# Memory keys of a cross-attention kept in DRAM between their making and their use

## Chip, core and metric

One Trainium2 chip, one core. The metric is the device time of one execution in microseconds (us), of which the median of several runs is taken. A profiled execution has a trace of every instruction beside it. Engines are named PE (TensorE), DVE (VectorE), ACT (ScalarE), POOL (GpSimd) and SP (SyncE, which here only issues transfers).

## What is computed

One decoder layer over 512 tokens of width 1024, in float32: a SwiGLU feed-forward block, a mixer (an SSD head group and a differential-attention head group that share one input and one output projection), a cross-attention into a memory of 256 rows, a second feed-forward block, a final norm. The part that the change touches is the cross-attention:

```python
def memory_cross_attention(h, mem_n, w_cq, w_ck, w_cv, w_co):
    bsz, seqlen, _ = h.shape
    mlen = mem_n.shape[1]
    q = (h @ w_cq).reshape(bsz, seqlen, CROSS_HEADS, CROSS_HEAD_DIM)
    k = (mem_n @ w_ck).reshape(bsz, mlen, CROSS_HEADS, CROSS_HEAD_DIM)
    v = (mem_n @ w_cv).reshape(bsz, mlen, CROSS_HEADS, CROSS_HEAD_DIM)
    logits = jnp.einsum('bqhd,bkhd->bhqk', q, k,
                        preferred_element_type=jnp.float32) * (CROSS_HEAD_DIM ** -0.5)
    p = jax.nn.softmax(logits, axis=-1)
    o = jnp.einsum('bhqk,bkhd->bqhd', p.astype(v.dtype), v).reshape(bsz, seqlen, D_MODEL)
    return o @ w_co
```

The keys `k` depend on the memory alone, so they can be made long before the queries.

## The kernel before

**Number format.** PE multiplies in a format (float32r) that keeps fewer bits. So nearly every operand is split into a high and a low part: ACT copies the value into the format (`hi`, line 155 or 159), DVE subtracts that from the value (`lo`, line 156 or 160). A product is three matmuls, hi x hi, hi x lo and lo x hi (`mm3`, which calls `mm`, line 146). Every weight tile is treated so as well: SP loads it raw (`wr`, six buffers, line 174), ACT and DVE split it (`wh`, `wl`, three buffers each).

**Tiles and pools.** Activations lie as tiles of 128 partitions by 512 float32 values (2 KB per partition). They come from one pool, `sp`, with 55 slots of that size (`NSLOT`); tiles of at most 1 KB have 16 slots of their own (`NHALF`). `s2(name)` asks for a tile. A new tile that finds no free slot waits until the last reader of an old one is done. PSUM has eight banks, four under the name `acc` and four under `aux`.

**Stages around the change**, with the times at which the trace shows them:

- 349 to 373 us: `memory_keys` multiplies the memory by `w_ck` into four PSUM banks, two key tiles of 256 columns in each (`pck`).
- 371 to 387 us: `keys_apart` (line 1080) scales each bank by the norm row of the memory into `ckf` (line 1083, DVE) and splits that into two tiles `ck`, a high and a low one. Four banks make eight tiles of 2 KB.
- 373 to 765 us: the mixer. Eight attention heads (`queries_keys`, `head`, `values`, `out_attn`) and four SSD groups (`group_dense`, `group`). The normed input, `hnh` and `hnl`, 16 tiles, is kept until the last gate projection `pz`. A step of its own, `steps` (line 656), turns the time-step projection `pdt` into decays: POOL loads two small constants, `ii` (line 660) and `hb` (line 662), PE turns the projection with `ii` (`pdk`), DVE adds a part of `hb` (line 668), POOL raises e to the other part (`ea`, line 684), DVE uses `ea` at line 685.
- 764 to 814 us: the last output tiles of the attention group and `memory_values`, which makes the values `cv` of the cross-attention (`pcv`).
- 805 to 850 us: `out_proj` multiplies the eight SSD outputs `ys` by the output weights, one output tile of 24 matmuls after the other. `upd_c` (line 1128) adds each to `x`, splits the result for the cross-attention (`h_c`) and sums its squares.
- 850 us on: `cross_dense` makes the queries of a head, `cross` reads `ck` (first at 867 us), and the head's softmax and value product follow.

Beside all this runs `block_sums_in_dram` (line 1243): SP copies weight blocks of the second feed-forward block inside DRAM and POOL adds others onto them (line 1260).

**What sets the order.** `Order` (line 57) runs generators. The dense ones (projections) follow one another; every matmul moves a planner's clock on by its columns plus 8 over 2400, for a tile of 512 columns 0.217 units. The others (`spawn`) are side chains: after each `yield n` a chain becomes due `n` units later and is run between two steps of a dense one. So the code comes out in one long list. SP and POOL execute their part of it exactly in that order:

```python
ctx.enter_context(tc.manual_schedule(engines={mybir.EngineType.SP, mybir.EngineType.Pool}))
```

PE, DVE and ACT get their order from the framework when the program is built: it runs the list through a simulated machine, takes what is ready there, earlier lines first, and hands out the slots of the pools on the way. On the chip every engine then keeps the order it was given.

`keys_apart` starts 1.0 unit after the last key matmul and yields 2.5 after each bank. `steps` starts when `steps_dense` is through, which follows the queries and keys of head 0.

Of the kernel before, what the change touches and what calls it, by code (L numbers as in the profile page):

```python
# [11 lines left out]
F32 = mybir.dt.float32  # L12
# [5 lines left out]
P = 128  # L18
T = 512
D = 1024  # L20
KT = D // P
NF = 22
MEM = 256
# [77 lines left out]
def body(tc, a, dbg=None):  # L101
    nc = tc.nc
# [8 lines left out]
    dram = ctx.enter_context(tc.tile_pool(name="dram", bufs=1, space=bass.MemoryType.DRAM))  # L111
# [3 lines left out]
    def nm(s):  # L115
        uid[0] += 1
        return f"{s}_{uid[0]}"

    def s2(s, dt=F32, shape=(P, T)):
        if math.prod(shape[1:]) <= T // 2:  # L120
            return sp.tile(list(shape), dt, tag="s1", name=nm(s), bufs=NHALF)
        return sp.tile(list(shape), dt, tag="s2", name=nm(s))
# [4 lines left out]
    def small(s, n, bufs=None):  # L127
        return tiny.tile([P, n], F32, tag=s, name=nm(s), bufs=bufs)
# [4 lines left out]
    def aux(s, shape=(P, T)):  # L133
        return aux_p.tile(list(shape), F32, tag="aux", name=nm(s))

    def dump(name, t):
        if dbg and name in dbg:
            nc.sync.dma_start(dbg[name], t.bitcast(F32) if t.dtype == R32 else t)
# [3 lines left out]
    od = Order()  # L142
# [5 lines left out]
    def transpose(out, x):  # L148
        od.t += 2 * (P + 8) / 2400
        nc.tensor.transpose(out, x, ident)  # L150

    def split_into(hi, lo, src, scale=None):
        if scale is None:
            return (
                S.activation(hi, src, AF.Copy),  # L155
                V.tensor_tensor(lo, src, hi.bitcast(F32), ALU.subtract),  # L156
            )
        return (
            S.activation(hi, src, AF.Copy, scale=scale),
            V.scalar_tensor_tensor(lo, src, scale, hi.bitcast(F32), ALU.mult, ALU.subtract),  # L160
        )

    def split(s, src, scale=None, half=False, n=T):
        if half:
            both = s2(s, R32, (P, 2, T // 2))
            hi, lo = both[:, 0], both[:, 1]
        else:
            hi, lo = s2(s + "h", R32, (P, n)), s2(s + "l", R32, (P, n))
        last[:] = [i.ins for i in split_into(hi, lo, src, scale)]
        return hi, lo  # L170
# [145 lines left out]
    def mm3(ps, w, x, first, last, wc=slice(None), xc=slice(None)):  # L316
        (wh, wl), (xh, xl) = w, x
        mm(ps, wh[:, wc], xh[:, xc], first, False)
        mm(ps, wh[:, wc], xl[:, xc], False, False)
        mm(ps, wl[:, wc], xh[:, xc], False, last)  # L320
# [92 lines left out]
    def make_h(k, c, x):  # L413
        return split("hm", x[k], par[:, c + k : c + k + 1])
# [601 lines left out]
    ck, cv = [], []  # L1016
# [52 lines left out]
    def memory_keys():  # L1069
        pairs = []  # L1070
        for n in range(0, KT, 2):
            ps = (aux, acc)[n // 4]("pck", (P, 2, MEM))
            for j in range(2):
                yield from proj(ps[:, j], load_w(a["wck"][n + j]), hm)
            pairs.append(ps)
        hm.clear()
        od.spawn(keys_apart(pairs), 1.0)
        yield lambda: len(h) == KT

    def keys_apart(pairs):  # L1080
        for ps in pairs:
            kf = s2("ckf", shape=(P, 2, MEM))
            V.tensor_tensor(kf, ps, st_mem.row[:, None, :].to_broadcast([P, 2, MEM]), ALU.mult)
            hi, lo = (s2("ck", R32, (P, 2, MEM)) for _ in range(2))
            split_into(hi, lo, kf)
            ck.extend((hi[:, j], lo[:, j]) for j in range(2))
            yield 2.5

    def memory_values():
        pv = [[acc("pcv") for _ in range(2)] for _ in range(2)]  # L1090
# [37 lines left out]
    def upd_c(o, po):  # L1128
        V.tensor_tensor(x[o], x[o], po, ALU.add)
        h_c.append(make_h(o, C_CROSS, x))  # L1130
        st_c.add(x[o])
        dump(f"x2_{o}", x[o])
        if o == KT - 1:
            h.clear()
            od.spawn(islice(st_c.finish(), 1), 3.0)
# [17 lines left out]
    od.add(out_attn(1, SPLIT, 8, True))  # L1153
    od.add(memory_values())
    od.add(out_proj(ys, a["wos"], lambda: all(y is not None for y in ys), upd_c))


    oc = [None] * 8

    def cross_dense(hd):  # L1160
        ps = [acc("pcq") for _ in range(2)]
        for j in range(2):
            yield from proj(ps[j], load_w(a["wcq"][2 * hd + j]), h_c)
        q = [split("cq", ps[j], 0.0625) for j in range(2)]
        od.spawn(cross(hd, q), W["c0"])

    def cross(hd, q):
        pth = [None, None]
        es = [None, None]
        for s in range(3):  # L1170
            if s < 2:
                ps = aux("pcs", (P, 2, MEM))
                for i in range(2):
                    for j in range(2):
                        qs = slice((2 * s + i) * P, (2 * s + i + 1) * P)
                        mm3(ps[:, i], q[j], ck[2 * hd + j], j == 0, j == 1, wc=qs)
                mx = small("cmx", 2)
                V.tensor_reduce(mx, ps, axis=AX.X, op=ALU.max, negate=True)
                col = st_c.col[:, 2 * s : 2 * s + 2]
                V.tensor_tensor(mx, mx, col, ALU.mult)  # L1180
                sm = small("csm", 2)
                e = es[s] = s2("ce", shape=(P, 2, MEM))
                for i in range(2):
                    S.activation(e[:, i], ps[:, i], AF.Exp, bias=mx[:, i : i + 1], scale=col[:, i : i + 1], accum_out=sm[:, i : i + 1])
                rc = small("crc", 2)
                V.reciprocal(rc, sm)
                for i in range(2):
                    V.tensor_scalar(e[:, i], e[:, i], rc[:, i : i + 1], None, ALU.mult)
                yield W["cs"]
            if s > 0:  # L1190
                e = es[s - 1]
                pt = aux("cpt", (P, 2, 2 * P))
                for kb in range(2):
                    for i in range(2):
                        transpose(pt[:, kb, i * P : (i + 1) * P], e[:, i, kb * P : (kb + 1) * P])
                pth[s - 1] = split("pth", pt.rearrange("p a b -> p (a b)"))
                yield W["ct"]
        for j in range(2):
            po = aux("pco")
            f = 2 * hd + j  # L1200
            for i2 in range(2):
                for kb in range(2):
                    mm3(po[:, i2 * 256 : i2 * 256 + 256], cv[kb][f // 4], pth[i2], kb == 0, kb == 1, wc=slice((f % 4) * P, (f % 4 + 1) * P), xc=slice(kb * 256, kb * 256 + 256))
            oc[f] = split("oc", po)
# [366 lines left out]
```

## Time and profile before

| | |
|---|---|
| median of three runs | 1307.42 us (1307.05 to 1309.1) |
| profiled execution | 1307.78 us, of which the span from first to last instruction is 1306.0 us |
| mean granted clock of PE | 0.997 |
| ACT busy | 706.9 us, 54% |
| POOL busy | 120.1 us, 9% |
| bytes moved by transfers | 234.75 MB, mean 180 GB/s |

In the lines of the profile a row such as `L156 DVE TENSOR_TENSOR ck<-ckf,ck x4` names the line of the code, the engine, the operation, the tile written, the tiles read and the count. `[3.96 <-PE pf L146]` behind a row says that the engine had been idle for 3.96 us before it and which event ended that. In the views of waits a row has the waiting instruction, what it waited for, and then the sum in us, the number of times and the longest. A matmul's end is modelled, since matmuls overlap; that PE is busy does not mean that it runs at its peak. Rows of a transfer give the time of its issue; its landing is listed apart.

### The profile page before, as it was taken

What the parts mean: (1) busy time and instruction counts of PE and PEld (TensorE: products, weight loads), DVE (VectorE), ACT (ScalarE), POOL (GpSimd) and SP (SyncE); (2) the same over time, 40 slices, a digit from 0 to 9 for tenths busy, and PEclk for the clock granted to TensorE, in tenths of its full rate; (3) what the DMA queues carried; (4) which work ended last, traced back from release to release, by engine and by line L of the source; (5) the groups of instructions that cost most, each with busy time, mean ns of one, the idle gap of its engine ahead of it and who ended that gap; (6) DMA issues with size and microseconds to landing.
All of it is one profiled execution on the core that took longest, in us unless ns stands there. A gap on an engine that the chain in (4) does not pass through costs nothing.

```text
span 1306.0 us, 20077 instructions
## 1 busy us (share of the span) xinstructions
PE 1288.3 (99%) x7709; PEld 1125.4 (86%) x7709; DVE 972.6 (74%) x1542; ACT 706.9 (54%) x1208; POOL 120.1 (9%) x149
## 2 busy tenths in 40 slices
PE   9999999999999999999999999999999999999997
PEld 7889998997887778777788878888889999989995
DVE  6987898798776676567867687645677878877886
ACT  7554564565754564346645465434365646555564
POOL 0001010001100011101012021020001000000000
PEclk9999999999999999999999999999999999999999
DMA  9367677877974525653475648684248876666653
GB/s 340 87 185 193 185 193 197 229 196 212 284 235 146 138 65 151 226 164 105 91 202 160 193 122 241 189 223 128 65 131 247 208 233 177 189 195 181 186 189 107
DMA packets 69263, 234.75 MB, mean 180 GB/s; under 512 B 8160, under 2 KB 9664, under 8 KB 68816
## 3 DMA queue, kind: packets, MB, share of 16 engines
q1 hardware_dynamic: 53200, 180.91, 41.8%
q0 software_dynamic: 13168, 45.67, 19.4%
q10 hardware_dynamic: 2800, 6.91, 1.6%
q8 instruction: 60, 0.98, 0.3%
q14 instruction: 35, 0.29, 0.1%
HBM read 231.30 MB, written 48.29 MB: 214 GB/s over the span
## 4 chain that ended last, share of the span: by engine, by line
PE 79%; issue 13%; DVE 3%; ACT 2%; POOL 1%; DMA 1%; ACTq 0%; POOLq 0%; DVEq 0%
PE qb L243 12%; PE pm L146 10%; PE qa L243 8%; PE qe L243 8%; PE ob L1294 5%; PE pxbc L146 4%; PE oa L1294 4%; PE oe L1294 3%; PE pcq L146 3%; PE pz L146 3%; PE pa L146 2%; PE pcv L146 2%; PE pg L146 2%; PE pu L146 2%; PE pq L146 2%
## 5 line engine op out<-in xcount | busy, mean ns | idle before, releaser
L155 ACT ACTIVATE wh<-wr 128x1024 fp32r<-128x1024 f32 (+1 forms) x323 | 328.2, 1018 | 331.9 <-issue 63.7
L156 DVE TENSOR_TENSOR wl<-wr,wh 128x1024 fp32r<-128x1024 f32 (+1 forms) x323 | 377.7, 1174 | 133.6 <-ACT wh L155 130.4
L771 ACT ACTIVATE ec<-ec,mn 128x512 f32<-128x512 f32 (+3 forms) x64 | 35.3, 554 | 33.7 <-DVE mn L770 33.7
L146 PE MATMUL pxbc<-hnh,wh 128*128 128x512 f32 x128 | 52.6, 411 | 0.0
L146 PE MATMUL pxbc<-hnh,wl 128*128 128x512 f32 x128 | 50.2, 392 | 0.0
L146 PE MATMUL pxbc<-hnl,wh 128*128 128x512 f32 x128 | 50.2, 392 | 0.0
L243 PE MATMUL qa<-hmh,wl 128*128 128x256 f32 x152 | 43.1, 284 | 0.1
L243 PE MATMUL qe<-s24h,wl 128*128 128x256 f32 x152 | 43.1, 284 | 0.0
L243 PE MATMUL qa<-h11h,wh 128*128 128x256 f32 x152 | 43.1, 283 | 0.0
L243 PE MATMUL qb<-s24h,wl 128*128 128x256 f32 x152 | 43.1, 283 | 0.0
L243 PE MATMUL qb<-s31h,wh 128*128 128x256 f32 x152 | 43.0, 283 | 0.0
L243 PE MATMUL qb<-s31l,wh 128*128 128x256 f32 x152 | 43.0, 283 | 0.0
L243 PE MATMUL qb<-s31h,wl 128*128 128x256 f32 x152 | 43.0, 283 | 0.0
L243 PE MATMUL qa<-h11h,wl 128*128 128x256 f32 x152 | 43.0, 283 | 0.0
L243 PE MATMUL qa<-hmh,wh 128*128 128x256 f32 x152 | 43.0, 283 | 0.0
L243 PE MATMUL qa<-h11l,wh 128*128 128x256 f32 x152 | 43.0, 283 | 0.0
L243 PE MATMUL qa<-hml,wh 128*128 128x256 f32 x152 | 43.0, 283 | 0.0
L243 PE MATMUL qb<-s24l,wh 128*128 128x256 f32 x152 | 43.0, 283 | 0.0
L243 PE MATMUL qe<-s24h,wh 128*128 128x256 f32 x152 | 43.0, 283 | 0.0
L243 PE MATMUL qe<-s24l,wh 128*128 128x256 f32 x152 | 43.0, 283 | 0.0
L243 PE MATMUL qb<-s24h,wh 128*128 128x256 f32 x152 | 43.0, 283 | 0.0
L243 PE MATMUL qb<-hml,wh 128*128 128x256 f32 x152 | 43.0, 283 | 0.0
(457 smaller groups left out, 4170.9 us busy)
## 6 DMA issues: line engine op xcount, KB each, us to landing
wr<-in_f2q SPq DMA_DIRECT2D x44, 512.0 KB, 4.5
wr<-in_f1q SPq DMA_DIRECT2D x40, 512.0 KB, 4.5
wr<-in_f1b SPq DMA_DIRECT2D x25, 512.0 KB, 6.3
isum<-in_f2q SPq DMA_DIRECT2D x22, 512.0 KB, 5.3
wr<-isum SPq DMA_DIRECT2D x22, 512.0 KB, 4.3
wsum<-in_f2b SPq DMA_DIRECT2D x20, 512.0 KB, 6.3
wr<-wsum SPq DMA_DIRECT2D x20, 512.0 KB, 4.9
wr<-in_f1q POOLq DMA_DIRECT2D x16, 512.0 KB, 6.9
```

The lines of the kernel that those rows point to most:

```text
L146: newest_mm[:] = [nc.tensor.matmul(out, w, x, start=start, stop=stop).ins]
L155: S.activation(hi, src, AF.Copy),
L156: V.tensor_tensor(lo, src, hi.bitcast(F32), ALU.subtract),
L243: newest_mm[:] = [nc.tensor.matmul(out, a_[:, wc], b_, start=first and f == 0 and kp == 0 and j == 0, stop=kp == n - 1 and j == 2, skip_gr ...
L771: S.activation(ec[:, :n], ec[:, :n], AF.Exp, bias=mn, scale=-1.0, accum_out=sm[c][:, i : i + 1])
L1294: newest_mm[:] = [nc.tensor.matmul(ps, a_[:, ts], b_[:, ws], start=first and k == 0 and j == 0, stop=k == n - 1 and j == 2, skip_group_che ...
```

## The change

The scaled keys `ckf` are no longer split when they are made. POOL stores each of the four tiles to a buffer in DRAM (`ck_d`), and the tile's slot is given back. When the second output tile of the SSD projection has been added to `x` (`o == 1` in `upd_c`), a new chain `keys_back` starts: SP loads the four tiles again, 3.0 units apart, and then each is split into its two `ck` tiles, 4.0 units apart. `cross` gets a test that holds it back while the keys are not all there. The keys' values and the matmuls that read them stay the same.

```diff
+    ck_d = [dram.tile([P, 2, MEM], F32, name=f"ck_d{n}") for n in range(4)]
+
     def keys_apart(pairs):
-        for ps in pairs:
+        for n, ps in enumerate(pairs):
             kf = s2("ckf", shape=(P, 2, MEM))
             V.tensor_tensor(kf, ps, st_mem.row[:, None, :].to_broadcast([P, 2, MEM]), ALU.mult)
+            nc.gpsimd.dma_start(ck_d[n], kf)
+            yield 2.5
+
+    def keys_back():
+        kf = []
+        for n in range(4):
+            kf.append(s2("ckf", shape=(P, 2, MEM)))
+            nc.sync.dma_start(kf[n], ck_d[n])
+            yield 3.0
+        for n in range(4):
             hi, lo = (s2("ck", R32, (P, 2, MEM)) for _ in range(2))
-            split_into(hi, lo, kf)
+            split_into(hi, lo, kf[n])
+            kf[n] = None
             ck.extend((hi[:, j], lo[:, j]) for j in range(2))
-            yield 2.5
+            yield 4.0
...
         dump(f"x2_{o}", x[o])
+        if o == 1:
+            od.spawn(keys_back())
...
     def cross(hd, q):
+        while len(ck) < KT:
+            yield 1.0
```

## Prediction

> **What bounds the kernel now.** I read the page first, then PE's waits between the making of the memory keys and their use, then the busy time by stage.
>
> ```profile
> span 1306.0 us, 20077 instructions
> PE 1288.3 (99%) x7709; PEld 1125.4 (86%) x7709; DVE 972.6 (74%) x1542; ACT 706.9 (54%) x1208; POOL 120.1 (9%) x149
> ```
>
> PE is busy for 1288.3 of 1306.0 us. Only what makes PE wait can move the end. These are all of PE's waits between 390 and 868 us, the stretch in which the keys lie idle:
>
> ```profile
> PE pot L150 <- DVE mn L770: 0.9, 1, 0.9
> PE pm L146 <- DVE x L857: 0.8, 1, 0.8
> PE pm L146 <- DVE wl L156: 0.6, 1, 0.6
> PE nrow L146 <- POOL ndiag L375: 0.5, 1, 0.5
> PE po L146 <- DVE wt L156: 0.3, 1, 0.3
> PE py L146 <- DVE th L971: 0.3, 1, 0.3
> PE pt L150 <- DVE on L840: 0.2, 1, 0.2
> ```
>
> Seven waits, 3.6 us in sum: that is all a gain can come from in this stretch. The stages show where they lie (columns: stretch, its length, then busy time of PE, PEld, DVE, ACT and POOL, granted clock, DMA share, GB/s):
>
> ```profile
> 365.00:390.00 25.00, 25.00 (x144) 20.22 (x143) 18.15 (x27) 12.68 (x18) 0.00 (x0) 1.00 0.75 240
> 735.00:760.00 25.00, 24.72 (x134) 19.85 (x134) 15.87 (x25) 12.23 (x24) 0.00 (x0) 1.00 0.43 138
> 760.00:815.00 55.00, 53.72 (x273) 42.95 (x273) 41.74 (x62) 31.43 (x55) 12.87 (x16) 1.00 0.66 198
> 815.00:850.00 35.00, 35.00 (x155) 28.57 (x154) 23.78 (x31) 16.49 (x23) 0.07 (x1) 1.00 0.70 192
> ```
>
> Where the keys are made (365 to 390) and where the SSD output is projected (815 to 850) PE is busy without a hole. Between 735 and 815 it loses 0.28 + 1.28 = 1.56 us.
>
> **What the change frees.** The eight tiles `ck` are written at 371 to 387 us and first read at 867:
>
> ```profile
> L146 PEld LDWEIGHTS pcs<-ck,cqh x64: 186/190/192, 867.5 to 918.2; 128*128 128x128 f32 x64
> ...
> L155 ACT ACTIVATE ck<-ckf x4: 613/623/634, 371.6 to 384.8; 128x512 fp32r<-128x512 f32 x4
> L156 DVE TENSOR_TENSOR ck<-ckf,ck x4: 684/688/693, 372.2 to 386.1; 128x512 fp32r<-128x512 f32 x4
> ```
>
> They hold 8 of the pool's 55 slots of 2 KB for about 480 us. That matters only while all 55 are taken. I laid the first and last use of every tile of this pool on one time line. Between the keys and the cross-attention the pool is full once, from 735.9 to 757.9 us. At 745 us it holds `ck` 8, `hnh`/`hnl` 16, `yah`/`yal` 8, `ysh`/`ysl` 8, `th2` 6, `hm` 4, `xdt` 2 and one each of `cbm`, `e2`, `conv`: 55. The trace shows what waits then:
>
> ```profile
> 743.75 1.06 ACT L155 ACTIVATE wh<-wr 128x1024 fp32r<-128x1024 f32 x1 [4.67 <-PE pxbc L146]
> 748.78 0.63 ACT L867 ACTIVATE th<-conv 128x512 f32<-128x512 f32 x1 [3.96 <-PE pf L146]
> ```
> ```profile
> 749.44 0.69 DVE L868 SCALAR_TENSOR_TENSOR th<-th,conv 128x512 f32<-128x512 f32 x1 [3.37 <-ACT th L867]
> 750.17 0.75 DVE L986 SCALAR_TENSOR_TENSOR y<-th,dskh,py 128x512 f32<-128x512 f32 x1
> ```
>
> The `th2` at 748.78 (the trace calls it `th`) reads a `conv` that is long finished and waits for PE's `pf`, which does not feed it: it wants the slot that the last reader leaves. `y` at 750.17 is a new tile too. So ACT loses 3.96 us and DVE 3.37 us to the full pool. With eight slots more both go away. PE feels it only as what DVE and ACT then catch up on. Its waits for `th` (L971, 0.3), for `x` (L857, 0.8) and for `ndiag` (0.5) sum to the 1.56 us that the stages show lost behind it. Bounds: a gain of 1.56 us, or none if all three stem from elsewhere. The wait for `x` at the output projection is probably a PSUM bank that DVE reads last and would remain; the other two, 0.8 us, I take as gone. What is late next is the bank.
>
> **The work that moves.** Four splits leave 371 to 387 us: 4 x 0.623 = 2.5 us of ACT and 4 x 0.688 = 2.75 us of DVE. PE had no hole there, so that is worth nothing. The same work comes back with the loads. Those are four of 256 KB on SP, with no arithmetic in front of them. SP runs far ahead, so they go out near the output weights that the code asks for around them, and the splits can start as soon as they land, about 800 us. The idle time there:
>
> ```profile
> 815.64 1.23 ACT L155 ACTIVATE ysh<-y 128x512 fp32r<-128x512 f32 x2 [8.46 <-DVE y L1010]
> ```
> ```profile
> 814.80 1.41 DVE L1010 SCALAR_TENSOR_TENSOR y<-y,par,nrow 128x512 f32<-128x512 f32 x2 [5.91 <-PE nrow L146]
> ...
> 839.60 0.69 DVE L1129 TENSOR_TENSOR x<-x,pm 128x512 f32<-128x512 f32 x1 [2.03 <-PE pm L146]
> ```
> ```profile
> 839.42 1.06 ACT L155 ACTIVATE wh<-wr 128x1024 fp32r<-128x1024 f32 x1 [3.25 <-issue]
> ```
> ```profile
> 790.90 4.83 SPq L174 DMA_DIRECT2D wr<-in_wos  x3
> ```
>
> ACT has 8.46 us and DVE 5.91 us in one piece before 815, and 3.25 and 2.03 us in every later output tile. I cost the splits at 0. If that cover were gone, the worst is 2.75 us of DVE in PE's way. Behind the loads on SP stand the output weights. The three issued from 790.90 on include those split at 818 and later, so a load that had to wait for its slot has over 20 us before anyone misses it: 0. The test `len(ck) < KT` never holds: the splits are due 24 planner units after output tile 1 and the first projection of the cross-attention starts after 6 more tiles of 24 x 520/2400 = 5.2 each, 31.2 units.
>
> **The wait that is added.** The four stores go on POOL, whose order is the order of the code. They are due 1.0, 3.5, 6.0 and 8.5 units after the keys. The `steps` chain is due after two projections of 5.2 and 16 more matmuls of 0.217, 13.9 units. So all stores stand ahead of its two small loads and its power on POOL, and of the sums in DRAM that are issued beside them. POOL today:
>
> ```profile
> 349.47 0.90 POOL L1260 DMA_DIRECT2D isum<-in_f2q  x1
> 350.07 0.83 POOL L660 DMA_DIRECT2D ii<-in_ii  x1
> 350.61 0.90 POOL L662 DMA_DIRECT2D hb<-in_hb  x1
> 357.67 3.75 POOL L684 TENSOR_TENSOR ea<-euler,hb 128x16 f32<-128x16 f32 x1 [6.16 <-DMA hb<-in_hb]
> ```
>
> All of this happens at 349 to 361 us now. After the change POOL must sit until DVE has written the fourth `ckf`:
>
> ```profile
> 379.51 1.23 DVE L156 TENSOR_TENSOR wl<-wr,wh 128x1024 fp32r<-128x1024 f32 x1 [3.12 <-ACT wh L155]
> 380.65 0.68 DVE L160 SCALAR_TENSOR_TENSOR ql<-pq,qh 128x512 fp32r<-128x512 f32 x1
> 381.25 0.68 DVE L1083 TENSOR_TENSOR ckf<-pck,row 128x512 f32<-128x512 f32 x1
> 382.64 0.69 DVE L156 TENSOR_TENSOR ck<-ckf,ck 128x512 fp32r<-128x512 f32 x1 [0.70 <-ACT ck L155]
> 383.25 0.68 DVE L1083 TENSOR_TENSOR ckf<-pck,row 128x512 f32<-128x512 f32 x1
> ```
>
> That is 383.25 + 0.68 = 383.9 as it stands. Without the `ck` operation between, the fourth follows the third and ends at 381.25 + 2 x 0.68 = 382.6. Issues on POOL stand 0.6 us apart. One store and one sum later, `ii` goes out at 383.8 to 385.1. Its user is PE:
>
> ```profile
> 393.75 1.06 PE L146 MATMUL pdk<-ii,dtf 32*128 32x16 f32 x8
> ```
> ```profile
> DMA to landing us min/median/max: 7.3/7.3/7.3
> ```
> ```profile
> isum<-in_f2q POOLq DMA_DIRECT2D x11, 512.0 KB, 7.8
> ...
> wr<-in_woa SPq DMA_DIRECT2D x16, 256.0 KB, 2.7
> ```
>
> The 7.3 us of `ii` already hold a sum in front of it on the same queue. It lands at 391.1 to 392.4, some 1.4 to 2.7 us before 393.75. A store of 256 KB from POOL is not in the trace. Beside `ii` it costs between 0 and 7.8 us, the landing of a POOL transfer of twice its size. I take 2.7, that of the 256 KB load, as the nearest in size. With the earlier `ckf` this gives 393.8, just in time: 0.0 us. With the later one it is 1.3 us late. The row for 7.8 gives at most 385.1 + 7.3 + 7.8 - 393.75 = 6.5 us. The power `ea` moves by as much and takes 3.75 us; DVE wants it 8 us after `pdk`, so it follows.
>
> [...]
>
> The sum: -0.8 (pool no longer full) + 0 (moved splits) + 0 (loads on SP) + 0.0 (POOL) = -0.8 us. The profiled execution took 1307.78 us, its span of 1306.0 and 1.8 around it; the median of the runs is 1307.42. Both move alike: 1306.6 us at the median.
>
> **The rivals.** A measurement of this kernel can tell about 0.2%, 2.6 us, from no change.
>
> *`ii` comes late and PE stands.* The mechanism is the one above; it decides from a landing after 393.75. If a store costs half of what a POOL sum of twice its bytes costs, 3.9 us, `ii` lands at 385.1 + 7.3 + 3.9 = 396.3 and PE stands for 2.5 us. A hole of that size has a second price here:
>
> ```profile
> 317.67 1.04 PE L1294 MATMUL ob<-wl,s24h 128*128 128x512 f32 x2 [2.48 <-DVE wl L156]
> ```
> ```profile
> 317.00:322.00 5.00, 4.33 (x12) 3.42 (x13) 3.70 (x6) 2.05 (x3) 4.20 (x5) 0.66 0.96 262
> ```
>
> After its hole of 2.48 us PE was granted 0.66 of its clock over 5 us, 5 x 0.34 = 1.7 us lost. Together 4.2 us: 1311.6. For it: the slack is 0 to 2.7 us. Against it: the order of PE, DVE and ACT is made by a simulated run that sees POOL's new order and can put `pdk` later.
>
> [...]
>
> *The new order brings other waits.* Any changed allocation reshuffles DVE, ACT and PE from 371 us on. If the seven waits doubled, +3.6: 1311.0. Nothing in the trace points to where.
>
> *All seven waits go.* Then 1307.4 - 3.6 = 1303.8. Against it: outside 735.9 to 757.9 the pool is never full, and four of the waits (0.9, 0.6, 0.3, 0.2) lie elsewhere.
>
> *The change frees nothing that counts.* SP fetches the keys back at about 790 us already, so the slots are free until then, not until 820. The full stretch lies before that, so this holds in part only; at worst 1307.4, no change.
>
> **How the numbers follow.** The forecast with its own bounds (-1.56 to +1.3) and the case that nothing counts stay within 2.6 us: 0.68. `ii` late: 0.13. Reshuffled waits: 0.09, of which all but a little lies over the bound. All waits gone: 0.10. So faster 0.10, same 0.68, slower 0.22. The range runs from 1304.8, half way between a full gain of 1.56 (1305.9) and the all-gone case (1303.8), to 1311.6, the price of the late `ii`.
>
> **What would show it.** Right: the pool's idle time before `th` L867 near 748 us is gone; PE's waits between 735 and 815 sum to about 0.8; POOL's `ii` is issued near 384; `ckf` comes back on SP near 790; the `ck` splits lie before 815 with PE at 35.00 of 35.00 afterwards. Wrong: PE waits at `pdk` for `ii` or at its first use of `hb`; a stretch below 1.00 of the clock near 395 us; waits of over 1 us in places where none was; splits of `ck` in front of a weight split that PE waits for.

## Result and profile after

The changed kernel takes 1309.81 us (median of 22 runs, 1307.34 to 1311.27), the kernel before beside it 1307.53 us (22 runs, 1304.84 to 1310.98). The ratio is 1.0015, with a 95% interval from 1.0009 to 1.0021: slower by about 2 us, where a small gain was forecast. Two executions ran far below the clock of the others and are left out of the times: the profiled one with the loads on POOL (mean granted clock 0.752), of which only the order of the instructions is read, and one of the kernel before (0.84).

The page of the profiled execution after:

```profile
span 1308.5 us, 20086 instructions
PE 1287.9 (98%) x7709; PEld 1125.1 (86%) x7709; DVE 971.9 (74%) x1542; ACT 706.6 (54%) x1208; POOL 121.5 (9%) x153
```

PE has as much work as before and 2.5 us more span. PE's waits between 390 and 868 us, the same view as in the prediction:

```profile
PE pm L146 <- ACT wh L155: 3.0, 1, 3.0
PE pot L150 <- DVE mn L770: 0.9, 1, 0.9
PE pm L146 <- DVE wl L156: 0.6, 1, 0.6
PE po L146 <- DVE wt L156: 0.3, 1, 0.3
PE pt L150 <- DVE on L840: 0.2, 1, 0.2
```

The three waits for `x`, `ndiag` and `th` are gone, all 1.6 us of them. In their place stands one of 3.0 us for a weight's high part. Busy time by stage (columns as in the prediction):

```profile
735.00:760.00 25.00, 25.00 (x140) 20.70 (x139) 21.60 (x34) 15.38 (x31) 0.00 (x0) 1.00 0.47 154
760.00:815.00 55.00, 55.00 (x286) 45.38 (x285) 38.57 (x55) 29.22 (x51) 12.42 (x16) 1.00 0.78 224
815.00:850.00 35.00, 31.96 (x127) 25.43 (x126) 22.25 (x29) 17.33 (x25) 0.00 (x0) 0.90 0.49 154
```

PE now runs without a hole from 735 to 815. It loses 3.04 us from 815 to 850, where it lost nothing before, and there its granted clock falls to 0.90: another 35 x 0.10 = 3.5 us, which the finer view in the last section puts at 3.4.

How much each side weighs shows in the distance from the first matmul of the memory keys (`pck`) to the first of the cross-attention's queries (`pcq`). It leaves out what varies from run to run ahead of the keys. Before (counts, shortest/median/longest in ns, first and last start):

```profile
L146 PE MATMUL pck<-hm,wh x128: 277/283/364, 349.1 to 372.7; 128*128 128x256 f32 x128
L146 PE MATMUL pcq<-hmh,wh x64: 388/389/478, 850.3 to 911.1; 128*128 128x512 f32 x64
```

After:

```profile
L146 PE MATMUL pck<-hm,wh x128: 278/283/383, 348.9 to 372.4; 128*128 128x256 f32 x128
L146 PE MATMUL pcq<-hmh,wh x64: 388/389/478, 852.3 to 913.2; 128*128 128x512 f32 x64
```

That is 501.2 us before and 503.4 after, 2.2 more. With 3.0 + 3.4 us lost in the output projection, some 4.2 us must have been won elsewhere: far more than the 0.8 of the forecast, and more than the 1.6 that the waits show.

**Where the new wait comes from.** ACT in the output projection, before:

```profile
818.56 2.01 ACT L155 ACTIVATE wh<-wr 128x1024 fp32r<-128x1024 f32 x2 [1.68 <-PE pm L146]
820.47 0.71 ACT L159 ACTIVATE hmh<-x,par 128x512 fp32r<-128x512 f32 x1
...
821.61 0.71 ACT L159 ACTIVATE hmh<-x,par 128x512 fp32r<-128x512 f32 x1
```

And after:

```profile
815.03 0.72 ACT L159 ACTIVATE hmh<-x,par 128x512 fp32r<-128x512 f32 x1 [2.59 <-DVE x L1142]
...
816.18 0.71 ACT L159 ACTIVATE hmh<-x,par 128x512 fp32r<-128x512 f32 x1
...
819.57 0.72 ACT L159 ACTIVATE hmh<-x,par 128x512 fp32r<-128x512 f32 x1 [2.16 <-DVE x L1142]
...
820.72 2.94 ACT L155 ACTIVATE wh<-wr 128x1024 fp32r<-128x1024 f32 x3
```

Before, ACT splits the weights of output tiles 3 and 4 first and then `x0` and `x1` (`hmh`). After, the splits of `x0`, `x1` and `x2` come first. The one of `x2` needs PE's product of tile 2, and only behind it stand three weight splits in one piece, those of tiles 3, 4 and 5. ACT sits idle for 2.59 and 2.16 us in front of work that it could not yet do, with work that it could do queued behind. PE finishes tile 2 and has no weight:

```profile
818.42 0.39 PE L146 MATMUL pm<-ysh,wl 128*128 128x512 f32 x1
821.81 0.79 PE L146 MATMUL pm<-ysh,wh 128*128 128x512 f32 x1 [3.00 <-ACT wh L155]
```

The weights were there long before. SP after:

```profile
786.26 0.34 SPq L174 DMA_DIRECT2D wr<-in_wos  x1
786.77 0.81 SPq L1093 DMA_DIRECT2D ckf<-ck_d  x2
788.00 0.33 SPq L174 DMA_DIRECT2D wr<-in_wos  x1
788.43 1.01 SPq L1093 DMA_DIRECT2D ckf<-ck_d  x2
791.05 0.33 SPq L174 DMA_DIRECT2D wr<-in_wos  x1
```

The weight of tile 3 is asked for at 788.00, between the loads of the keys, over 30 us before its split; these weights land after 5.8 us in the median. So on the chip nothing came late; it is the order built into ACT's program that keeps the split back. The weights that are split late are those whose load stands behind the first key load on SP.

### The profile page after: what moved, and what is told of

It reads as the page before. It is cut to its first block, busy times and chain, and to the rows that moved or that the text cites. A ratio compares the mean times of both kernels' runs of the same rounds, so it can differ in the third digit from the quotient of the medians.

```text
span 1308.5 us, 20086 instructions
## 1 busy us (share of the span) xinstructions
PE 1287.9 (98%) x7709; PEld 1125.1 (86%) x7709; DVE 971.9 (74%) x1542; ACT 706.6 (54%) x1208; POOL 121.5 (9%) x153
## 5 line engine op out<-in xcount | busy, mean ns | idle before, releaser
L243 PE MATMUL qb<-hmh,wh 128*128 128x256 f32 x152 | 43.0, 283 | 0.0
L243 PE MATMUL qb<-hmh,wl 128*128 128x256 f32 x152 | 43.0, 283 | 0.0
```

What stands on the lines that cost most here:

```text
L243: newest_mm[:] = [nc.tensor.matmul(out, a_[:, wc], b_, start=first and f == 0 and kp == 0 and j == 0, stop=kp == n - 1 and j == 2, skip_gr ...
```

## Experiments

**Theory.** The freed slots win about 4.2 us. The loads of the keys on SP tip the built order on ACT, and that costs 6.4 us in the profiled execution. **Rivals.** The loads, the splits or the stores cost the time themselves; the gain is an accident of one execution or comes from the work that left ACT and DVE.

| kernel | median us | ratio to before, 95% interval | `pck` to `pcq`, us |
|---|---|---|---|
| before | 1307.53 | 1 | 501.2 |
| changed | 1309.81 | 1.0015 [1.0009, 1.0021] | 503.4 |
| stores only | 1308.45 | 1.0001 [0.9992, 1.0010] | 501.1 |
| loads on ACT | 1303.74 | 0.9968 [0.9956, 0.9979] | 497.0 |
| before, order damaged | 1313.88 | 1.0045 [1.0033, 1.0058] | 506.4 |
| order repaired | 1305.72 | 0.9984 [0.9975, 0.9993] | 498.9 |
| loads on ACT, slots held | 1307.95 | 1.0002 [0.9991, 1.0013] | 501.3 |
| keys back at tile 3 | 1309.34 | 1.0017 [1.0006, 1.0028] | 503.3 |
| loads on POOL | 1304.31 | 0.9973 [0.9963, 0.9984] | - |
| keys back early | 1308.78 | 1.0006 [0.9996, 1.0016] | 502.1 |
| tiles of their own | 1304.01 | 0.9974 [0.9965, 0.9983] | 496.9 |
| 51 slots | 1308.68 | 1.0011 [1.0002, 1.0020] | 502.5 |

The kernel before was run again beside each group: 1308.1 us for the first four experiments, 1307.53 for the next four, 1307.55 for the last two.

**Stores only.** Two lines on top of the kernel before; the eight key tiles stay where they were:

```diff
+            nc.gpsimd.dma_start(ck_d[n], kf)
             hi, lo = (s2("ck", R32, (P, 2, MEM)) for _ in range(2))
```

> This is the kernel before with the four stores on POOL alone: each pair of key tiles is written to DRAM and still split at once, nothing is loaded back, and the eight key tiles sit in their slots as before. Theory (the time is lost where three weight splits stand behind the splits of x0 to x2 on ACT, and part of it is won back by the eight freed slots): neither is here, so 1307.5 us within 0.4, the three holes of TensorE between 735 and 781 (1.56 us) still there, no hole near 821. Rival P (the stores on POOL and the later ii cost the time): about 1309.8, with a wait of TensorE at pdk.

Measured: 1308.45, which is 0.55 us over the range given, but so was the kernel before beside it (1308.1): the ratio is 1.0001, no change. The holes near 755, 768 and 780 are still there. The stores cost nothing that can be told, though they pushed `ii` to 385.48 us.

**Loads on ACT.** One word of the changed kernel:

```diff
-            nc.sync.dma_start(kf[n], ck_d[n])
+            nc.scalar.dma_start(kf[n], ck_d[n])
```

> The changed kernel with one word altered: the four loads are issued from ACT, not from SP. In the built order the weight splits of output tiles 3 and 4 then stand ahead of the split of x0 again, as in the kernel before. Theory: the gain of the freed slots stays (TensorE enters the output projection 4.4 us earlier than before) and the hole of 3.0 us near 821 with its 6.8 us of half clock is gone: 1303.5 us, between 1302.8 and 1304.6. Rival L (the four loads and eight splits themselves cost the time, on the DMA engines or on ACT and DVE): 1309 or more, as in the changed kernel. Rival N (the 4.4 us were an accident of the one profiled execution): 1307.5.

Measured: 1303.74. Busy time by stage:

```profile
735.00:760.00 25.00, 25.00 (x139) 20.70 (x138) 21.92 (x35) 15.15 (x30) 0.00 (x0) 1.00 0.46 151
760.00:815.00 55.00, 55.00 (x287) 45.40 (x286) 38.26 (x56) 29.77 (x52) 12.41 (x16) 1.00 0.72 205
815.00:850.00 35.00, 35.00 (x156) 28.79 (x154) 26.72 (x35) 19.23 (x28) 0.00 (x0) 1.00 0.68 219
```

Stores, loads and splits are all still there, and PE has no hole. So they cost nothing that shows here; what costs is the order. From `pck` to `pcq` it is 4.2 us shorter than the kernel before.

**Before, order damaged.** The kernel before, with three weight splits tied behind the split of `x2`:

```diff
-            yield from proj(po, load_w(wts[o]), src)
+            with behind(list(x_split.get(2, [])) if src is ys and o in (3, 4, 5) else []):
+                w = load_w(wts[o])
+            yield from proj(po, w, src)
...
         h_c.append(make_h(o, C_CROSS, x))
+        x_split[o] = list(last)
```

> The kernel before, keys split at once and kept, with no store and no load: only the splits of the weights of output tiles 3 to 5 are tied behind the split of x2 on their engines, which gives on ACT the order that the changed kernel has. Theory: the same hole of TensorE of about 3.0 us at the first product of tile 3 and about 6.8 us of half clock behind it, so 1307.5 + 6.4 = 1313.9 us, between 1313.0 and 1314.6; if the hole comes without the half clock, 1310.5. Rival L (loads and splits cost the time): 1307.5, no hole.

Measured: 1313.88, 5.8 us more. Its waits:

```profile
PE pm L146 <- ACT wh L155: 2.5, 1, 2.5
PE pm L146 <- DVE wl L156: 1.2, 2, 0.6
```

No key is stored or loaded here, and the loss is there. The order alone makes it. The number is the one that I gave, but in the profiled execution its parts are not: the waits grew by 2.5 + 0.6 us, and half clock cost 1.7 us in place of 3.4, together 4.8 of the 5.2 us that `pck` to `pcq` is longer.

**Order repaired.** The changed kernel with its loads on SP among the same weights. The weight of tile `o + 3` is asked for and split before the update of tile `o`, and the split of `x[o]` is tied behind it:

```diff
             yield from proj(ps[o], ws[o], src, range(6, 8))
+            if src is ys:
+                if o == 0:
+                    early = {2: load_w(wts[2])}
+                    kf = []
+                kf += [keys_load(2 * o), keys_load(2 * o + 1)]
+                early[o + 3] = load_w(wts[o + 3])
+                next_w[:] = recent
             update(o, ps[o])
...
-        h_c.append(make_h(o, C_CROSS, x))
+        with behind(list(next_w)):
+            h_c.append(make_h(o, C_CROSS, x))
```

> The changed kernel with its loads on SP between the same output weights (one key load pair behind the load of tile 2, one behind that of tile 3), but the weight splits of tiles 3, 4 and 5 are made before the splits of x0, x1 and x2 and those are tied behind them. Theory: no hole near 821, the gain of the slots stays, 1303.5 us, between 1302.8 and 1304.8. Rival L (it is the loads on SP between the weights, or the splits, that cost): 1309 or more. Rival N (no real gain from the slots): 1307.5.

Measured: 1305.72, faster than both kernels but 0.9 us over the range. The hole of 3 us is gone and a smaller one has come:

```profile
PE pm L146 <- DVE wl L156: 2.1, 2, 1.5
```

My ties put ACT in order and left DVE with a new one: DVE stands 4.75 us in front of an addition to `x` at 826.96, with the low part of the next weight behind it. It is the same fault on the other engine.

**Loads on ACT, slots held.** Are the 4.2 us the slots'? Eight empty tiles are taken beside the stores. They were to be given up near 770; in the trace that happens at 792 to 803 us:

```diff
             nc.gpsimd.dma_start(ck_d[n], kf)
+            for _ in range(2):
+                held.append(s2("held", shape=(P, 2, MEM)))
+                V.memset(held[-1][:, 0, :1], 0.0)
...
+        with behind(attn_done):
+            for t in held:
+                V.tensor_copy(gone, t[:, 0, :1])
+        held.clear()
```

> The kernel with the loads on ACT (1303.74 us), in which eight slots of the pool of 55 are taken again: eight empty tiles are allocated where the kernel before had its eight key tiles (beside each store, one element set) and given up after the last attention update of x, near 770. Theory (the gain comes from the slots): the holes near 755, 768 and 780 come back, 1.56 us, and so does the 2.5 us by which the matmuls between 735 and 815 took longer: 1307.7 us, between 1306.8 and 1308.5. Rival R (the gain comes from the work that left ACT and DVE near 375): 1303.7, no holes. In between, by the holes alone: 1305.3.

Measured: 1307.95, the gain is gone whole, and the three holes are back at 755.13, 768.15 and 779.88 us. Yet they sum to 1.55. The other 2.6 us lie in time that counts as busy. The matmuls of `py` in the kernel with held slots (the columns are those of the stages, for this tile alone):

```profile
735.00:815.00 80.00, 5.66 (x64) 3.97 (x64) 2.97 (x4) 1.00 0.59 179
```

And with the slots free, loads on ACT:

```profile
735.00:815.00 80.00, 4.38 (x64) 3.41 (x64) 2.96 (x4) 1.00 0.64 188
```

The same 64 matmuls, 5.66 us against 4.38. The timeline of the kernel before shows where (it also has 5.66):

```profile
755.14 0.43 PE L146 MATMUL py<-th,xdt 128*64 128x128 f32 x2 [0.28 <-DVE th L971]
755.50 0.50 PE L146 MATMUL pz<-hnh,wh 128*128 128x512 f32 x1
...
757.31 1.09 PE L146 MATMUL py<-th,xdt 128*64 128x128 f32 x14
758.33 0.50 PE L146 MATMUL pz<-hnl,wh 128*128 128x512 f32 x1
```

With the loads on ACT they come in one piece:

```profile
748.98 1.09 PE L146 MATMUL py<-th,xdt 128*64 128x128 f32 x16
```

In one piece sixteen records take 1.09 us. Broken off after two, the two take 0.43 and the other fourteen 1.09 again, and for every break one more of the large matmuls, here `pz`, takes 0.50 in place of 0.39. Three of the four groups of `py` are broken so before, none with the loads on ACT. Only the break at 755 has a wait on the chip, the 0.28 us for `th`; the pieces at 783 and 793 us have none. So it is the order given when the program is built that breaks them; that it does so because the inputs come late in the simulated run was not observed. A full pool thus costs PE also where it is never idle. `py` accounts for 1.28 of the 2.6 us; the rest is spread over other matmuls of the stretch and was not taken apart.

**Keys back at tile 3.** `if o == 3:` in place of `if o == 1:`, nothing else.

> The changed kernel with keys_back started two output tiles later (o == 3 in place of o == 1), loads on SP as in the change. In the built order the weight splits of output tile 5 and the next three then stand behind the split of x4. Theory (whatever weight is loaded behind the first key load is split late, wherever the key loads are put): the hole at 821 is gone and one of about 3 us comes at the first product of tile 5, near 832, with 2 to 3.4 us lost to half clock: 1309.3 us, between 1308.5 and 1310.5. Rival C (only the place near tile 3 is bad): 1303.7, no hole.

Measured: 1309.34. The hole has moved to tile 5, as said:

```profile
829.29 0.72 ACT L159 ACTIVATE hmh<-x,par 128x512 fp32r<-128x512 f32 x1 [4.19 <-DVE x L1142]
...
830.44 2.93 ACT L155 ACTIVATE wh<-wr 128x1024 fp32r<-128x1024 f32 x3
```

The stall followed the loads of the keys to their new place.

**Loads on POOL.** `nc.gpsimd.dma_start(kf[n], ck_d[n])` for the loads.

> The changed kernel with the four loads issued from POOL in place of SP. In the built order the weight splits of tiles 3 and 4 stand ahead of the split of x0, as with the loads on ACT. Theory: 1303.7 us, between 1302.8 and 1304.8, no hole of TensorE between 735 and 860. Rival Q (POOL's accumulating transfers stand before the loads and the keys come late): a wait of TensorE at pcs near 864, 1305 or more.

Measured: 1304.31. On ACT two weight splits stand ahead of the split of `x0` again. So both queues tried other than that of the weights do.

**Keys back early.** `keys_back` starts with the memory values (`od.spawn(keys_back(), 20.0)` in `memory_values`), loads on SP.

> The changed kernel with keys_back started at the beginning of the memory values, loads on SP among the last loads of the values' weights. In the built order the weight splits of tiles 3 and 4 stand ahead of the split of x0, the first key split comes before the split of ysh and the other three between those of x0 to x2. Theory: no hole of 3 us, 1303.7 us for the same slots; the three key splits stand ahead of the weight splits of tiles 5 and 6, 1.3 us of ACT each, against a product of 5.4 us for each tile, so up to 1 us of waits: 1304.2, between 1303.0 and 1305.5. Rival E (the eight slots are taken again too early, and the holes near 755 to 780 come back): 1305.3 to 1307.7.

Measured: 1308.78, and neither theory's number. No hole between 735 and 780 came back, so rival E is out. But I had looked at the order around `x0` only. The first key load now stands in front of the weights of the last values and of output tiles 0 and 1, and it is tile 0 that is late:

```profile
PE pm L146 <- ACT wh L155: 1.7, 1, 1.7
PE pm L146 <- DVE wl L156: 1.2, 2, 0.6
```

The rule held, and I had not applied it. PE lost 2.6 us of waits here, 0.35 of them at the last values, and 1.7 us of half clock; 0.7 us of the distance to the kernel with the loads on ACT stays unexplained.

**Tiles of their own, and 51 slots.** What about the loads turns the order? In the first of these two the loads stay on SP where the change has them but land in four tiles outside the shared pool, which is cut to 51 slots for that. The second has the cut alone.

```diff
-NSLOT = 55
+NSLOT = 51
...
-            kf.append(s2("ckf", shape=(P, 2, MEM)))
+            kf.append(cp.tile([P, 2, MEM], F32, name=f"ckb{n}"))
```

> The changed kernel with its loads on SP where the change has them, but the four tiles that they land in are tiles of their own, not slots of the shared pool; the pool is cut from 55 slots to 51 to make room. In the built order the weight splits of tiles 3 and 4 stand ahead of the split of x0 again. Theory (it is the loads' claim on slots of the shared pool, ahead of the weights' loads in SP's order, that turns the order on ACT): no hole near 821, at most 51 slots were ever taken after the change, so the gain stays: 1303.7 us, between 1302.8 and 1304.8. Rival S (the loads' place on SP delays the weights whatever they land in): 1309.5, hole of 3 us.

> The changed kernel with the pool cut from 55 slots to 51 and nothing else: the control for the run with tiles of their own. The built order on ACT is that of the changed kernel. Theory: 51 slots are enough, the hole near 821 stays: 1309.7 us, between 1308.8 and 1310.6. If the smaller pool costs or wins something by itself, the difference from 1309.81 shows it.

Measured: 1304.01 and 1308.68. With tiles of their own SP's stream is the one of the change (a weight, two key loads, a weight, two key loads), and ACT has the old order:

```profile
817.38 2.01 ACT L155 ACTIVATE wh<-wr 128x1024 fp32r<-128x1024 f32 x2 [1.62 <-PE pm L146]
819.29 0.71 ACT L159 ACTIVATE hmh<-x,par 128x512 fp32r<-128x512 f32 x1
```

With 51 slots and the loads still in the pool, the wait for `wh` is 3.0 us again (its median lies 0.1 us under the range I gave). So it is neither the loads' place on SP nor their transfers, but their claim on a slot of the shared pool, ahead of the weights' loads. The run that builds the order hands out slots on the way and keeps SP's order; a load that it holds up for a slot holds up the weights behind it, and it then takes `x0` to `x2` first on ACT. These last steps are argued, not shown: the run that builds the order was not observed, neither that a load waited in it nor for which release. By the expectation above no more than 51 slots were ever taken after the change, and 51 slots give the same hole as 55, so a plain lack of slots on the chip does not explain it. On the chip the loads did not wait.

## Why the prediction was wrong, step by step

- *The pool no longer full, -0.8 us.* The mechanism was right, the size was not: 4.2 us in the traces, 3.4 to 4.2 us by the ratios of the three kernels without the hole (0.9974, 0.9973, 0.9968). ACT's wait of 3.96 us for a slot, before `th` at 748.78, is gone. In the changed kernel the same instruction comes 8 us earlier and waits only for the `conv` that it reads:

```profile
740.63 0.63 ACT L867 ACTIVATE th<-conv 128x512 f32<-128x512 f32 x1 [1.86 <-DVE conv L879]
```

  I expected the wait for `x` to remain as a PSUM bank; it went with the others. And I priced only waits, while 2.6 us more lay in matmuls that the profile counts as busy. So the seven waits were not "all a gain can come from", and the bound of 1.56, which rests on the same reason, was wrong.
- *The moved splits, 0.* The price was right, the place was not. I expected them before 815 us; they run from 832.6 to 850.4, one per output tile:

```profile
L155 ACT ACTIVATE ck<-ckf x4: 614/616/617, 832.6 to 849.0; 128x512 fp32r<-128x512 f32 x4
L156 DVE TENSOR_TENSOR ck<-ckf,ck x4: 683/684/685, 834.0 to 850.4; 128x512 fp32r<-128x512 f32 x4
```

  No wait of PE belongs to them, here or with the loads on ACT.
- *The loads on SP, 0.* This is the step that failed. I argued that "a load that had to wait for its slot has over 20 us before anyone misses it". On the chip that is true. But the order of PE, DVE and ACT is settled beforehand, and the claim on the slot counted there. In the profiled execution it cost 6.4 us, 3.0 of wait and 3.4 of half clock. Over all runs the clock part is smaller: the mean granted clock is 0.9955 in the 22 runs of the changed kernel and 0.9974 in 35 of the kernel before, and 0.0019 of 1306 us is 2.5 us. That makes 5.5 us on average, an estimate.
- *The stores on POOL, 0.0.* Right. `ii` was forecast at 383.8 to 385.1, which the trace misses by 0.2 us, and PE's `pdk` to be just in time:

```profile
371.55 1.21 POOL L1086 DMA_DIRECT2D ck_d<-ckf  x2 [21.98 <-DVE ckf L1085]
381.91 1.14 POOL L1086 DMA_DIRECT2D ck_d<-ckf  x2 [9.16 <-DVE ckf L1085]
383.04 0.94 POOL L1277 DMA_DIRECT2D isum<-in_f2q  x1
383.62 0.90 POOL L660 DMA_DIRECT2D ii<-in_ii  x1
```
```profile
ck_d<-ckf POOLq DMA_DIRECT2D x4, 256.0 KB, 5.9
...
ii<-in_ii POOLq DMA_DIRECT2D x1, 2.0 KB, 8.2
```

  It lands at 383.62 + 8.2 = 391.8, and `pdk` starts at 393.49 without a wait. Behind the stores the landing took 8.2 us instead of 7.3, 0.9 us more where I took 2.7. The store itself lands after 5.9 us.
- *The rivals.* The late `ii` did not come. "The new order brings other waits" did, at 0.09 and with the remark that nothing pointed to where. Something did: the rows of SP, with weight loads behind the place where the key loads would go, and a built order that I knew to depend on slots. That the freed slots count for nothing was wrong, and that all seven waits go was too: three went, and more was won than the 3.6 us of all seven.

The sum that the two profiled executions support: -4.2 from the slots, 0 for stores, loads and splits, +6.4 for the order, +2.2 us in all. That 1309.81 lies inside the stated range is luck: its upper end was the price of a late `ii`, and `ii` was in time.

## What to carry to other kernels

Where the order of an engine is settled when the program is built, a transfer that costs nothing on the chip can still turn that order, through the slot that it claims ahead of others in its queue. Give such a load a queue or a tile of its own, and read the changed order of every engine before pricing the change by idle time. And a busy PE is no bound on a gain: the built order can also break small matmuls into pieces, which only their own busy time shows.

## What the runs showed of the hardware

The same kind of hole in PE costs its clock or not. Between 314 and 321 us each of the eleven traces that are read for times has a hole, and what followed it (from the granted clock over 316 to 328 us) came in steps of 1.7 us lost: none in four of the traces, one step in six, two in the damaged order. Holes of nearly one length differ in it: none followed 2.60 us in the changed kernel, one step followed 2.48 in the kernel before and 2.59 with tiles of their own. In the output projection the clock was at half over 6.8 us after the hole of 3.00:

```profile
821.00:822.00 1.00, 0.19 (x1) 0.19 (x2) 0.89 (x3) 1.00 (x2) 0.00 (x0) 0.70 0.00 0
822.00:828.00 6.00, 5.96 (x14) 4.18 (x15) 3.29 (x3) 1.65 (x2) 0.00 (x0) 0.50 0.60 207
828.00:829.00 1.00, 1.00 (x6) 0.83 (x5) 0.00 (x0) 0.00 (x0) 0.00 (x0) 0.89 0.94 360
```

That is 0.30 + 3.0 + 0.11 = 3.4 us lost, two steps, and again two in the kernel with the keys back at tile 3. The damaged order, the early loads and the 51 slots, with holes of 1.7 to 3.0 us there, lost one step each; the repaired order, with one of 1.46, lost none. So in these traces a hole of 1.7 to 3.0 us cost 0, 1.7 or 3.4 us on top. The spread among the runs of one kernel, 6.1 us for the kernel before (22 runs) and 1.8 for the loads on ACT (7 runs), is not explained by it: of the changed kernel's runs the slowest, 1311.27, had a mean clock of 0.996 and one of the fastest, 1307.81, had 0.995. What decides which hole costs the clock no run here shows.
